# Feed-forward and output projections turned from features-on-partitions to tokens-on-partitions in a two-layer streaming trunk

## The chip, the cores and the metric

The kernel runs on one core of one Trainium2 chip. The metric is device microseconds for one execution, the median of three runs. The engines are named as in the profile: PE is TensorE's matmul, PEld its weight load, DVE VectorE, ACT ScalarE, POOL GpSimd, SP SyncE. SP and ACT also issue DMAs here.

## The reference

Two layers over 256 tokens of 2048 features, all in float32. Layer 0 is a gated and a pooled mixer, layer 1 a latent attention; each is followed by a gated feed-forward layer of 5632 hidden features. Everything but the matrix products that follow here is the same before and after.

```python
for layer in range(DEPTH):                     # 2
    h = rmsnorm(x, g_mix[layer])               # x: 256 x 2048
    if layer % 2 == 0:                         # mixers; w_out_ab is 2048 x 2048
        p = h @ w_in_ab[i]
        mix = concatenate([a, b]) @ w_out_ab[i]
    else:                                      # attention; w_out_c is 2048 x 2048
        mix = mla(h, w_in_c[i], ..., w_out_c[i], cos, sin)
    x = x + mix
    h = rmsnorm(x, g_ffn[layer])
    # w_gate, w_up: 2048 x 5632, w_down: 5632 x 2048
    x = x + (silu(h @ w_gate[layer]) * (h @ w_up[layer])) @ w_down[layer]
return rmsnorm(x, g_final)
```

## The kernel before

**Precision.** Every weight and every activation that meets it is held as two float32r parts whose sum is the float32 value. A weight is loaded as `raw` (1 MB a load), ACT copies it to `wh` (L90) and DVE subtracts to get `wl` (L91), 1024 columns at a time. `raw` has 3 buffers, `wh` and `wl` 4 each. Activations lie the same way, the high part in the first 256 columns of a tile, the low part in the next 256 (`split_into`, L145). A product is wh x hi + wh x lo + wl x hi.

**The form before (`column`, L95).** The trunk `x` and all activations have features on the 128 partitions and the 256 tokens along the columns. One 128 x 128 block of weights stands in the array, and the activations move through it: one matmul of 512 columns (wh against hi and lo side by side, L113) and one of 256 (wl against hi, L114). This pair is the unit of work; the last pair of a sum has the two the other way round (L110, L111). A column tile is 16 pairs (22 for half of a down projection) and gives 128 output features for all tokens. `gather_halves` (L137) adds the two halves that stand in PSUM.

**The other form (`token_major`, L205),** used before for the attention's values only (`w_v1`) and written out by hand for the gated mixer's v (L239 to L261): 128 tokens of an activation stand in the array and 512 weight columns move. For one 128-row slice of the weights and one half of the tokens it takes three matmuls of 512 columns: hi against wh, hi against wl, lo against wh (L217 to L219).

**Stages.** The mixer v (to 53 us), the other mixer inputs, the output projection `w_o0` (16 column tiles), the feed-forward of layer 0 (two halves of 22 hidden tiles, each gate and up column by column, then 16 column tiles of the down projection), the latent attention (its products of `w_ckv`, `w_kr` and `w_cq` by `column`), the output projection `w_o1`, the second feed-forward, the final norm. `residual` (L187) adds a column tile of PSUM to `x`, writes the split input `xs` of the next product and the squares for the norm. The norm's factor is applied to the result of the product: `rstd_of` sums squares over partitions by a matmul, `spread` lays the factor along the columns by another. The engines run their own rows in order; a scheduler lays down that order when the kernel is built, and semaphores connect the engines.

Of the kernel before, what the change touches and what calls it, by code (L numbers as in the profile page):

```python
# [11 lines left out]
ALU = mybir.AluOpType  # L12
# [5 lines left out]
KD = D // P            # 16 feature tiles of the trunk  # L18
DFF = 5632
NF = DFF // P          # 44 feature tiles of the feed-forward layer  # L20
HALF = NF // 2
# [4 lines left out]
SPLIT = 1024           # weights split at a time, per partition  # L26
# [3 lines left out]
def trunk(ctx: ExitStack, tc: tile.TileContext, a: dict, out: bass.AP):  # L30
# [14 lines left out]
    x = big.tile([P, KD, T], F32, name="x")  # L45
    xs = big.tile([P, KD, 2 * T], F32R, name="xs")

# [4 lines left out]
    cnt = const.tile([P, 16], F32, name="cnt")  # L52

# [15 lines left out]
    # the table of activation functions is fetched while the first loads are under way  # L69
    warm = const.tile([P, 1], F32, name="warm")  # L70
    nc.scalar.activation(out=warm, in_=ones[:, 0:1], func=AF.Gelu_apprx_tanh)
    # and the tensor engine's clock is brought up
# [5 lines left out]
    def split_weights(src, n):  # L78
        """[P, n] of DRAM as pairs of tiles whose sum is exactly the weights."""
        raw = raws.tile([P, 2 * SPLIT], F32, name="raw")  # L80
        nc.sync.dma_start(out=raw[:, :n], in_=src)
        return split_raw(raw, n)
# [12 lines left out]
    def column(w, nk, moving):  # L95
        """One 128-column tile of a product, transposed: [128, (hi + cross | lo)] in PSUM."""
        ps = ps_mm.tile([P, 2 * T], F32, name="mm")
        k = 0
        for o in range(0, nk * P, 2 * SPLIT):
            n = min(2 * SPLIT, nk * P - o)  # L100
            for wh, wl, m in split_weights(w[:, o:o + n], n):
                for j in range(m // P):
                    product(ps, wh[:, j * P:(j + 1) * P], wl[:, j * P:(j + 1) * P], moving[:, k, :], k == 0, k == nk - 1)
                    k += 1
        return ps

    def product(ps, wh, wl, mv, first, last):
        """wh x (hi | lo) into the two halves, wl x hi into the first; the matmul that ends the sum covers both."""
# [7 lines left out]
    def short_product(ps, wh, wl, mv, first, last):  # L116
        """As product(), all of it in ps[:, :T]: for sums of few terms, where adding halves would weigh."""
# [4 lines left out]
    def columns(w, nk, nm, moving):  # L122
        """Column tiles whose weights share a load: w is [P, nm * nk * 128]."""
# [13 lines left out]
    def gather_halves(ps, name):  # L137
        """ps[:, :T] + ps[:, T:] in SBUF."""
# [6 lines left out]
    def split_into(dst, src, scale=None):  # L145
        """dst[:, :T] + dst[:, T:] = src (times a gain per partition), both parts in float32r."""
# [8 lines left out]
    def add_square(acc, src, first):  # L155
        if first:
            nc.scalar.activation(out=acc, in_=src, func=AF.Square)
        else:
            sq = tmp.tile([P, T], F32, name="sq")
# [3 lines left out]
    def rstd_of(accs, n):  # L163
        """(mean + eps) ** -0.5 of sums of squares (over partitions and over accs), per token on the
        partitions. spread() lays it along the free axis, the same on every partition."""
# [21 lines left out]
    def residual(m, ps, g, acc):  # L187
        """x tile m += product; then what the next layer needs of it."""
        t = tmp.tile([P, T], F32, name="rs")
        nc.vector.tensor_tensor(out=t, in0=ps[:, :T], in1=x[:, m, :], op=ALU.add)  # L190
        nc.vector.tensor_tensor(out=x[:, m, :], in0=ps[:, T:], in1=t, op=ALU.add)  # L191
        if g is None:
            return
        if g == "final":
            if m == KD - 1:
                # the last squares go into the sum over partitions by themselves
                nc.scalar.activation(out=last_sq, in_=x[:, m, :], func=AF.Square)
            else:
                add_square(acc, x[:, m, :], m == 0)
            nc.scalar.activation(out=fin[:, m, :], in_=x[:, m, :], func=AF.Copy, scale=gain("final", m))  # L200
        else:
            split_into(xs[:, m, :], x[:, m, :], gain(g, m))
            add_square(acc, x[:, m, :], m == 0)

    def token_major(w, nk, ncols, moving, evict):  # L205
        """Products with tokens on the partitions: w is [ncols/512][P, nk, 512]."""
        for c in range(ncols // 512):
            pss = [ps_mm.tile([P, 512], F32, name="mm") for _ in range(2)]
            for k0 in range(0, nk, 4):
                parts = split_weights(w[c, :, k0 * 512:(k0 + 4) * 512], 2048)  # L210
                for k in range(k0, k0 + 4):
                    wh, wl, _ = parts[(k - k0) // 2]
                    s = slice((k - k0) % 2 * 512, (k - k0) % 2 * 512 + 512)
                    for t in range(2):
# [4 lines left out]
                        nc.tensor.matmul(pss[t], lhsT=lo, rhs=wh[:, s], start=False, stop=k == nk - 1)  # L219
            for t in range(2):  # L220
                evict(c, t, pss[t])
# [7 lines left out]
    # x times the final gain, and the squares of its last tile  # L229
    fin = last_sq = None  # L230

# [1 line left out]
    # the gated mixer's v, tokens on the partitions; its loads alternate with those of x  # L233
    vg = att.tile([P, 2, 1024], F32, name="ckv")
    vss = stat.tile([P, 2, 2], F32, name="vss")
    sums = big.tile([P, 8, T], F32, name="hid")
    acc, sq = sums[:, :4, :], sums[:, 4:, :]
    pss = [[ps_mm.tile([P, 512], F32, name="mm") for t in range(2)] for c in range(2)]
    for k0 in range(0, KD, 2):  # L239
        raw = raws.tile([P, 2 * SPLIT], F32, name="raw")  # L240
        if k0 == 0:
            for k in range(2):
                nc.sync.dma_start(out=x[:, k, :], in_=a["x"][:, k, :])
                for c in range(2 * k, 2 * k + 2):
                    nc.sync.dma_start(out=raw[:, c * 512:(c + 1) * 512], in_=a["w_v0"][0][:, c * 512:(c + 1) * 512])
        else:
            nc.sync.dma_start(out=x[:, k0:k0 + 2, :], in_=a["x"][:, k0:k0 + 2, :])
            nc.sync.dma_start(out=raw, in_=a["w_v0"][k0 // 2])
        step = SPLIT if k0 else 512
        for k in (k0, k0 + 1):  # L250
            split_into(xs[:, k, :], x[:, k, :], gain("mix0", k))
# [368 lines left out]
```

## Time and profile before

| | before |
|---|---|
| median of three runs | 2015.97 us (2014.3 to 2018.14) |
| span of the profiled execution | 2013.7 us |
| PE busy | 1998.8 us, 99% of the span |
| DVE / ACT busy | 64% / 49% |
| mean granted TensorE clock | 0.997 of full speed |
| HBM traffic | 364 MB read, 182 GB/s |

The span runs from the first to the last instruction. The time of the profiled execution beyond its span is not listed; the fastest of the three runs is 0.6 us above the span, the median 2.3 us. A matmul's listed duration overlaps its neighbours, so what it costs in a row of matmuls is the distance from one start to the next.

### The profile page before, as it was taken

What the parts mean: (1) busy time and instruction counts of PE and PEld (TensorE: products, weight loads), DVE (VectorE), ACT (ScalarE), POOL (GpSimd) and SP (SyncE); (2) the same over time, 40 slices, a digit from 0 to 9 for tenths busy, and PEclk for the clock granted to TensorE, in tenths of its full rate; (3) what the DMA queues carried; (4) which work ended last, traced back from release to release, by engine and by line L of the source; (5) the groups of instructions that cost most, each with busy time, mean ns of one, the idle gap of its engine ahead of it and who ended that gap; (6) DMA issues with size and microseconds to landing.
All of it is one profiled execution on the core that took longest, in us unless ns stands there. A gap on an engine that the chain in (4) does not pass through costs nothing.

```text
span 2013.7 us, 28325 instructions
## 1 busy us (share of the span) xinstructions
PE 1998.8 (99%) x11436; PEld 1740.6 (86%) x11436; DVE 1291.6 (64%) x1899; ACT 987.8 (49%) x1440; POOL 7.4 (0%) x22
## 2 busy tenths in 40 slices
PE   9999999999999999999999999999999999999997
PEld 7888888888888888888899988888888888888886
DVE  6787666666556666666676767666665566666654
ACT  6554454444334455444455655544543345554442
POOL 0000000000000000000000000000000000000000
PEclk9999999999999999999999999999999999999998
DMA  7565555555556555555555245555555565555553
GB/s 278 170 209 186 189 188 183 186 182 177 182 188 201 188 188 188 175 175 191 196 184 167 85 161 182 182 187 188 188 169 192 179 202 183 188 186 187 173 187 121
DMA packets 60179, 368.11 MB, mean 183 GB/s; under 512 B 6928, under 2 KB 8720, under 8 KB 19344
## 3 DMA queue, kind: packets, MB, share of 16 engines
q1 hardware_dynamic: 58320, 364.93, 55.0%
q8 instruction: 89, 1.46, 0.3%
q10 hardware_dynamic: 1728, 1.37, 0.2%
q14 instruction: 42, 0.34, 0.0%
HBM read 364.18 MB, written 2.10 MB: 182 GB/s over the span
## 4 chain that ended last, share of the span: by engine, by line
PE 97%; DVE 1%; DMA 1%; ACT 0%; issue 0%; SPq 0%; POOLq 0%; DVEq 0%; ACTq 0%
PE mm L113 56%; PE mm L114 28%; PE mm L111 3%; PE mm L110 2%; PE mm L119 1%; PE mm L120 1%; PE mm L118 1%; PE mm L260 1%; PE mm L261 1%; PE sm L466 1%; PE mm L259 1%; DMA raw<-in_w_v 1%; PE sm L465 0%; PE mm L218 0%; PE mm L219 0%; PE mm L217 0%
## 5 line engine op out<-in xcount | busy, mean ns | idle before, releaser
L91 DVE TENSOR_TENSOR wl<-raw,wh 128x1024 fp32r<-128x1024 f32 (+2 forms) x708 | 844.7, 1194 | 420.6 <-ACT wh L90 414.2
L113 PE MATMUL mm<-xs,wh 128*128 128x512 f32 x3015 | 1073.3, 399 | 0.0
L90 ACT ACTIVATE wh<-raw 128x1024 fp32r<-128x1024 f32 (+2 forms) x708 | 731.9, 1034 | 561.3 <-PE mm L113 322.1
L114 PE MATMUL mm<-xs,wl 128*128 128x256 f32 x3015 | 846.2, 281 | 0.0
L113 PEld LDWEIGHTS mm<-xs,wh 128*128 128x128 f32 x3015 | 566.5, 188 | 129.8
L113 PE MATMUL mm<-hid,wh 128*128 128x512 f32 x1824 | 648.8, 399 | 0.0
L114 PEld LDWEIGHTS mm<-xs,wl 128*128 128x128 f32 x3015 | 569.3, 189 | 8.8
L114 PE MATMUL mm<-hid,wl 128*128 128x256 f32 x1824 | 512.6, 281 | 0.0
L113 PEld LDWEIGHTS mm<-hid,wh 128*128 128x128 f32 x1824 | 342.7, 188 | 80.2 <-DVE hid L149 0.3
L114 PEld LDWEIGHTS mm<-hid,wl 128*128 128x128 f32 x1824 | 344.5, 189 | 4.6
L140 ACT ACTIVATE half<-mm 128x256 f32<-128x256 f32 x201 | 77.2, 384 | 373.3 <-PE mm L111 373.3
L142 DVE TENSOR_TENSOR su<-mm,half 128x256 f32<-128x256 f32 x88 | 37.4, 425 | 95.3 <-ACT half L140 95.3
L142 DVE TENSOR_TENSOR sg<-mm,half 128x256 f32<-128x256 f32 x88 | 37.4, 424 | 90.5 <-ACT half L140 90.5
L111 PE MATMUL mm<-xs,wh 128*128 128x512 f32 x201 | 80.3, 400 | 0.0
L190 DVE TENSOR_TENSOR rs<-mm,x 128x256 f32<-128x256 f32 x96 | 40.8, 424 | 46.9 <-PE mm L111 46.9
L110 PE MATMUL mm<-xs,wl 128*128 128x256 f32 x201 | 56.7, 282 | 0.0
L148 ACT ACTIVATE hid<-su 128x256 fp32r<-128x256 f32 x88 | 37.0, 420 | 39.4 <-DVE su L387 39.4
L110 PEld LDWEIGHTS mm<-xs,wl 128*128 128x128 f32 x201 | 37.8, 188 | 10.2
L191 DVE TENSOR_TENSOR x<-mm,rs 128x256 f32<-128x256 f32 x96 | 40.7, 424 | 3.3
L387 DVE TENSOR_TENSOR su<-su,sg 128x256 f32<-128x256 f32 x88 | 37.4, 425 | 3.3
L386 DVE TENSOR_TENSOR su<-su,rstd 128x256 f32<-128x256 f32 x88 | 37.4, 424 | 3.0
L383 DVE TENSOR_TENSOR sg<-sg,rstd 128x256 f32<-128x256 f32 x88 | 37.3, 424 | 2.9
(146 smaller groups left out, 1111.3 us busy)
## 6 DMA issues: line engine op xcount, KB each, us to landing
raw<-in_w_gu SPq DMA_DIRECT2D x176, 1024.0 KB, 5.1
raw<-in_w_d SPq DMA_DIRECT2D x64, 1024.0 KB, 4.9
raw<-in_w_o SPq DMA_DIRECT2D x32, 1024.0 KB, 4.9
raw<-in_w_d SPq DMA_DIRECT2D x64, 384.0 KB, 3.1
raw<-in_w_v SPq DMA_DIRECT2D x11, 1024.0 KB, 6.7
raw<-in_w_z SPq DMA_DIRECT2D x8, 1024.0 KB, 4.9
raw<-in_w_u SPq DMA_DIRECT2D x8, 1024.0 KB, 4.9
raw<-in_w_q SPq DMA_DIRECT2D x6, 1024.0 KB, 4.9
```

Source lines behind the costliest of these rows:

```text
L90: nc.scalar.activation(out=wh[:, :m], in_=raw[:, o:o + m], func=AF.Copy)
L91: nc.vector.tensor_tensor(out=wl[:, :m], in0=raw[:, o:o + m], in1=wh[:, :m].bitcast(F32), op=ALU.subtract)
L110: nc.tensor.matmul(ps[:, :T], lhsT=wl, rhs=mv[:, :T], start=False, stop=False)
L111: nc.tensor.matmul(ps, lhsT=wh, rhs=mv, start=False, stop=True)
L113: nc.tensor.matmul(ps, lhsT=wh, rhs=mv, start=first, stop=False)
L114: nc.tensor.matmul(ps[:, :T], lhsT=wl, rhs=mv[:, :T], start=False, stop=last)
L140: nc.scalar.activation(out=c, in_=ps[:, T:], func=AF.Copy)
L142: nc.vector.tensor_tensor(out=s, in0=ps[:, :T], in1=c, op=ALU.add)
L190: nc.vector.tensor_tensor(out=t, in0=ps[:, :T], in1=x[:, m, :], op=ALU.add)
L191: nc.vector.tensor_tensor(out=x[:, m, :], in0=ps[:, T:], in1=t, op=ALU.add)
L386: nc.vector.tensor_tensor(out=su, in0=su, in1=r, op=ALU.mult)
L387: nc.vector.tensor_tensor(out=su, in0=su, in1=sg, op=ALU.mult)
```

## The change

The gate, up, down and both output projections go over to the tokens-on-partitions form; the products of layer 1's inputs (`w_ckv`, `w_kr`, `w_cq`) and the mixer inputs keep the old one. The trunk `x` becomes [128 tokens, 2 halves, 2048]. What a product takes must still have features on the partitions, so the results are transposed on PE: `turned` makes four 128 x 128 float32 transposes into one PSUM tile, and ACT and DVE split them from there. These calls wait in a list, `pending`, and one is taken after each load of weights (four slices of 128 rows) in `token_major`, or after each fourth pair in `column`. The norm's sums now come from the squaring activation's accumulator, per token, so that `rstd_of` and `spread` leave the feed-forward layers and the end. The input comes a second time as `xt`, tokens on partitions (2 MB), and the final gain as a row broadcast to all partitions (1 MB), both issued by ACT. A feed-forward layer is cut into 6 and 5 blocks of 512 hidden features.

```diff
-    def token_major(w, nk, ncols, moving, evict):
-        for c in range(ncols // 512):
+    def token_major(w, k0, nk, blocks, moving, evict):
+        for c in blocks:
             pss = [ps_mm.tile([P, 512], F32, name="mm") for _ in range(2)]
...
                     for t in range(2):
                         hi = moving[:, k, t * P:(t + 1) * P]
                         lo = moving[:, k, T + t * P:T + (t + 1) * P]
                         nc.tensor.matmul(pss[t], lhsT=hi, rhs=wh[:, s], start=k == 0, stop=False)
                         nc.tensor.matmul(pss[t], lhsT=hi, rhs=wl[:, s], start=False, stop=False)
                         nc.tensor.matmul(pss[t], lhsT=lo, rhs=wh[:, s], start=False, stop=k == nk - 1)
+                next_pending()
+            evict(c, pss)
+
+    def turned(src, put):
+        pt = ps_sm.tile([P, 512], F32, name="sm")
+        for j in range(2):
+            for t in range(2):
+                o = j * T + t * P
+                nc.tensor.transpose(pt[:, o:o + P], src(t, j), ident)
+        put(pt)
+
+    def into_trunk(w, k0, nk, moving, g, sums):
+        def evict(c, pss):
+            s = slice(c * 512, (c + 1) * 512)
+            for t in range(2):
+                nc.vector.tensor_tensor(out=x[:, t, s], in0=pss[t], in1=x[:, t, s], op=ALU.add)
+            if g is None:
+                return
+            for t in range(2):
+                sq = qpool.tile([P, 512], F32, name="qr")
+                nc.scalar.activation(out=sq, in_=x[:, t, s], func=AF.Square, accum_out=sums[:, t, c:c + 1])
+            if g == "final":
+                for t in range(2):
+                    nc.vector.tensor_tensor(out=x[:, t, s], in0=x[:, t, s], in1=gfin[:, s], op=ALU.mult)
+                return
+            for m in (4 * c, 4 * c + 2):
+                def put(pt, m=m):
+                    for j in range(2):
+                        split_into(xs[:, m + j, :], pt[:, j * T:(j + 1) * T], gain(g, m + j))
+                pending.append(lambda m=m, put=put: turned(lambda t, j: x[:, t, (m + j) * P:(m + j + 1) * P], put))
+        token_major(w, k0, nk, range(4), moving, evict)
...
+    nc.scalar.dma_start(out=gfin, in_=a["g_final"].broadcast_to([P, D]))
+    nc.scalar.dma_start(out=x, in_=a["xt"])
...
-    for m in range(KD):
-        residual(m, column(a["w_o0"][m], KD, ab), "ffn0", acc)
+    into_trunk(a["w_o0"], 0, KD, ab, "ffn0", sums)
...
-                pg = column(wgu[f, :, 0:D], KD, xs)
-                pu = column(wgu[f, :, D:2 * D], KD, xs)
...
+                def evict_gate(c, pss):
+                    for t in range(2):
+                        sg = qpool.tile([P, 512], F32, name="qn")
+                        nc.scalar.activation(out=sg, in_=pss[t], func=AF.Silu, scale=r[:, t:t + 1])
+                        gate.append(sg)
+                def evict_up(c, pss, hid=hid, at=at):
+                    hd = att.tile([P, 2, 512], F32, name="ckv")
+                    for t in range(2):
+                        nc.vector.scalar_tensor_tensor(out=hd[:, t, :], in0=pss[t], scalar=r[:, t:t + 1], in1=gate[t],
+                                                       op0=ALU.mult, op1=ALU.mult)
+                    for m in (0, 2):
...
+                        pending.append(lambda m=m, put=put: turned(lambda t, j: hd[:, t, (m + j) * P:(m + j + 1) * P], put))
+                token_major(wg, 0, KD, [c], xs, evict_gate)
+                token_major(wu, 0, KD, [c], xs, evict_up)
+            into_trunk(wd, 4 * at, 4 * n, hid, g_next if part else None, after)
...
-    rps = spread(rstd_of([acc, last_sq], D))
+    r = trunk_rstd(feed_forward(1, sums, "final"))
+    for t in range(2):
+        for o, n in ((0, 512), (512, 512), (1024, 1024)):
+            y = x[:, t, o:o + n]
+            if o < 1024:
+                nc.vector.tensor_scalar(out=y, in0=y, scalar1=r[:, t:t + 1], scalar2=None, op0=ALU.mult)
+            else:
+                nc.scalar.activation(out=y, in_=y, func=AF.Copy, scale=r[:, t:t + 1])
+            nc.sync.dma_start(out=out[:, t, o:o + n], in_=y)
```

Three places in the order of the instructions follow; an x and a number behind a row count equal rows that follow each other.

On PE, in the first feed-forward layer before, the join of two column tiles of a down projection:

```order
L114 MATMUL mm<-hid,wl 128x256
L110 MATMUL mm<-hid,wl 128x256
L111 MATMUL mm<-hid,wh 128x512
L113 MATMUL mm<-hid,wh 128x512
L114 MATMUL mm<-hid,wl 128x256
```

On PE in the changed kernel, the first load of a down projection's first block (24 matmuls) ends, and the four transposes of the last hidden block (`ckv` is the buffer that holds it) stand ahead of the second load:

```order
L211 MATMUL mm<-wl,hid 128x512
L212 MATMUL mm<-wh,hid 128x512
L222 MATMUL sm<-ident,ckv 128x128 x4
L210 MATMUL mm<-wh,hid 128x512
L211 MATMUL mm<-wl,hid 128x512
```

The 512 and 256 column pairs with weights in the array gave way to threes of 512 columns, and 68 such groups of four transposes have come in.

On ACT before, two hidden tiles of a feed-forward layer (`wh` the split of weights, `half` the gathering of gate and up, `sg` the gate's activation, `hid` the split of the result):

```order
L90 ACTIVATE wh<-raw 128x1024
L384 ACTIVATE sg<-sg 128x256
L90 ACTIVATE wh<-raw 128x1024
L140 ACTIVATE half<-mm 128x256
L90 ACTIVATE wh<-raw 128x1024
L148 ACTIVATE hid<-su 128x256
```

On ACT now, a gate and an up block of 512 hidden features (`qn` the gate's activation, read from the gate's PSUM; `hid` the split of two transposed tiles, read from the transposes' PSUM):

```order
L94 ACTIVATE wh<-raw 128x1024 x3
L417 ACTIVATE qn<-mm,rtok 128x512 x2
L94 ACTIVATE wh<-raw 128x1024 x11
L429 ACTIVATE hid<-sm 128x2x256
L94 ACTIVATE wh<-raw 128x1024 x2
L429 ACTIVATE hid<-sm 128x2x256
```

Of the 8 splits of the up block three now stand ahead of the gate's activation, which waits for the end of the gate block; before, such a wait came with every column tile, about every second split.

On ACT before, the first rows of the kernel that touch loads:

```order
L271 DMA rope_c<-in_rope_c 128x256
L90 ACTIVATE wh<-raw 128x512 x2
L151 ACTIVATE xs<-x,gains 128x256
L272 DMA rope_s<-in_rope_s 128x256
L90 ACTIVATE wh<-raw 128x512 x2
```

And now (`gfin` the broadcast final gain; the 2 MB of `x<-in_xt` follow eleven rows further on, after eight of the sixteen slices' `xs`):

```order
L304 DMA rope_c<-in_rope_c 128x256
L94 ACTIVATE wh<-raw 128x512 x2
L162 ACTIVATE xs<-hid,gains 128x256
L305 DMA rope_s<-in_rope_s 128x256
L94 ACTIVATE wh<-raw 128x512
L306 DMA gfin<-in_g_final 128x2048
L94 ACTIVATE wh<-raw 128x512
```

The broadcast of 1 MB has moved in among the first splits of weights, while the first loads of weights are under way.

## Rows read from the trace of the kernel before

**Rows 1.** The page's first part: busy time, share of the span, instructions.
```profile
PE 1998.8 (99%) x11436; PEld 1740.6 (86%) x11436; DVE 1291.6 (64%) x1899; ACT 987.8 (49%) x1440; POOL 7.4 (0%) x22
```

**Rows 2.** The chain that ended last, shares by engine; then PE's longest wait after 1172 us.
```profile
PE 97%; DVE 1%; DMA 1%; ACT 0%; issue 0%; SPq 0%; POOLq 0%; DVEq 0%; ACTq 0%
...
PE sm L169 <- ACT ssq_q L197: 1.3, 1, 1.3
```

**Rows 3.** Windows 500 to 800 us, L113's, then L111's matmuls: length, PE, PEld, clock, DMA.
```profile
500.00:800.00 300.00, 284.94 (x802) 150.62 (x802) 1.00 0.58 190
500.00:800.00 300.00, 19.20 (x48) 9.12 (x48) 1.00 0.58 190
```

**Rows 4.** Timeline of PE, tokens-on-partitions products: mixer v, then attention's values (start, duration).
```profile
15.87 0.40 PE L261 MATMUL mm<-wh,xs 128*128 128x512 f32 x1
...
52.61 0.39 PE L261 MATMUL mm<-wh,xs 128*128 128x512 f32 x1
...
1066.57 0.40 PE L217 MATMUL mm<-wh,ckv 128*128 128x512 f32 x1
...
1088.35 0.28 PE L118 MATMUL mm<-hid,wh 128*128 128x256 f32 x1
```

**Rows 5.** The attention's transposes (L486): their durations, and PE's timeline around two of them.
```profile
L486 PE MATMUL sm<-ident,pr x48: 270/272/315, 1102.2 to 1166.0; 128*128 128x128 f32 x48
...
1163.40 0.40 PE L113 MATMUL mm<-hid,wh 128*128 128x512 f32 x1
1163.64 0.27 PE L486 MATMUL sm<-ident,pr 128*128 128x128 f32 x1
1163.66 0.37 PE L114 MATMUL mm<-hid,wl 128*128 128x256 f32 x1
1163.87 0.38 PE L486 MATMUL sm<-ident,pr 128*128 128x128 f32 x2
1164.01 0.47 PE L113 MATMUL mm<-hid,wh 128*128 128x512 f32 x1
1164.32 0.28 PE L114 MATMUL mm<-hid,wl 128*128 128x256 f32 x1
```

**Rows 6.** Timeline of ACT at a block's end in the attention's values: start, duration, idle before.
```profile
1076.99 1.37 ACT L456 ACTIVATE xs<-mm,rtok 128x512 f32<-128x512 f32 x2 [0.98 <-PE mm L219]
1078.26 1.05 ACT L90 ACTIVATE wh<-raw 128x1024 fp32r<-128x1024 f32 x1
```

**Rows 7.** Groups of DVE and ACT, shapes apart: busy, mean ns of one, idle before.
```profile
L91 DVE TENSOR_TENSOR wl<-raw,wh 128x1024 fp32r<-128x1024 f32 x636 | 777.8, 1224 | 331.3 <-ACT wh L90 325.0
L304 DVE TENSOR_TENSOR pa<-qn 128x512 f32<-128x512 f32 x4 | 2.8, 694 | 0.1
L283 ACT ACTIVATE qr<-ckv 128x512 f32<-128x512 f32 x4 | 2.5, 634 | 0.0
```

**Rows 8.** The chain that ended last, 53 to 60 us: a sum of squares, a spread factor.
```profile
53.00 0.34 PE sm L169 x4
59.10 0.44 PE sm L179 x4
```

**Rows 9.** A window (length, PE, PEld, DVE, ACT, POOL, clock, DMA, GB/s), then the chain there.
```profile
10.00:15.00 5.00, 4.62 (x20) 3.52 (x19) 1.35 (x3) 2.87 (x4) 0.00 (x0) 1.00 1.01 379
...
6.54 6.52 DMA raw<-in_w_v
13.16 1.07 ACT wh L90
```

**Rows 10.** Timeline of the end: last add, POOL's power, store issues; then stores' KB and landing.
```profile
2000.40 0.42 DVE L190 TENSOR_TENSOR rs<-mm,x 128x256 f32<-128x256 f32 x1 [5.98 <-PE mm L111]
2003.03 0.69 POOL L173 TENSOR_TENSOR rtok<-rstd_v,mhalf 128x2 f32<-128x2 f32 x1 [742.50 <-DVE rstd_v L171]
2005.48 4.65 SPq L536 DMA_DIRECT2D out<-xs  x6
...
out<-xs SPq DMA_DIRECT2D x3, 512.0 KB, 2.9
```

## What I predicted, before the changed kernel ran

> **What bounds the kernel now.** I read the page's busy times first: PE is busy 99% of the span, DVE 64%, ACT 49% [rows 1]. Then the chain of waits that ended last: 97% of it is PE, and from 1172 us on PE waits longest for the last squares, 1.3 us at the very end [rows 2]. So a stage costs what its matmuls cost on PE, and whatever ACT, DVE or a load needs is hidden as long as it stays ahead. DMA is at 0.58 in the feed-forward, with the granted clock at 1.00, full speed [rows 3]. The edit must therefore be judged by PE's time per unit of product, then by what is new on PE, then by places where a cover could go.
>
> **The products.** The listed duration of a matmul (about 0.4 us for 512 columns) overlaps the next one, so the price is the distance between starts. Before, windows 500 to 800 us hold 802 pairs by L113 and 48 by L111, 850 pairs in 300 us: 0.353 us a pair [rows 3]. This includes every join of two column tiles. The changed form is in the trace twice. The mixer v has 163 matmuls from 15.87 to 52.61 us, 162 distances, 0.2268 us each; the attention's values have 96 from 1066.57 to 1088.35 us, 0.2269 each [rows 4]. The first has the same xs in the array as the gate and up products will have, the second has four block ends in it, so a join makes it no longer.
> Pairs that change: two output projections of 16 x 16 blocks (512) and six feed-forward products of 16 x 44 (4224), 4736 in all. They took 4736 x 0.353 = 1671.8 us. Four pairs (128 rows by 512 outputs, 256 tokens) become six matmuls of 512 columns: 4736 / 4 x 6 = 7104, x 0.2268 = 1611.2 us. **Saved: 60.6 us.** The number of columns that move is equal (4 x 768 = 6 x 512 = 3072); what goes is one instruction in four, 9472 to 7104.
>
> **The transposes.** There are 68 groups of four: 44 for 22 hidden blocks, 24 for three passages of the trunk into a next product. That is 272. Row L486 lists 0.272 us for the same instruction, but again the start distances count: from L113 at 1163.40 to L114 at 1164.32 are 0.92 us, in which stand two L113, one L114 and three transposes; a pair is 0.353, an L113 alone some 0.235, so three transposes took 0.92 - 0.353 - 0.235 = 0.33 us, 0.11 each, in the middle of float32r matmuls of both sizes [rows 5]. 272 x 0.11 = **29.9 us added**. Bounds: 0.10 to 0.16 each (the upper one a little over half of the listed duration, if a group cost something at its two ends), 27 to 44 us.
>
> **What leaves PE besides.** Two feed-forward layers lose a sum (0.34) and a spread (0.44), the entry of layer 1 a sum [rows 8]: **1.9 us saved**.
>
> **Joins and waits.** The new waits are ACT's gate activation and DVE's up product, which wait for a block's end with later splits queued behind them in order, and PE's transposes, which wait for DVE's result. At a block's end three splits of the next block stand ahead of the gate's activation, so PE has 1.5 loads, 36 matmuls or 8.2 us, in hand. In the attention's values the same happens: ACT waits 0.98 us for the end of a block, evicts in 1.37 us and then splits [rows 6], and the distance there stayed 0.2269. Per 24 matmuls (5.44 us) DVE has two splits of 1.224 us and ACT two of 1.05, plus four operations of 512 columns at some 0.69 in eight such stretches [rows 6, 7], about half of the time. The transposes come 5.4 us after a block's end; two DVE operations of 0.69 are done after 1.5. So nothing is late and I put these at nothing; if the cover were gone, each of 68 blocks would pay up to a split by ACT and DVE, 2.3 us. The load rate rises from 1 MB in 16 pairs (5.65 us) to 1 MB in 5.44, DMA from 0.58 to 0.60: no bound.
> One place is tighter: layer 1's entry, where `column` takes its first transposes 1.4 us after the down projection ends and needs the split tiles at its 13th pair, 4.2 us plus 0.9 of transposes later. DVE's two adds (1.4), ACT's two squares (0.64 each) and four splits of 0.4 to 0.5 with a weight split between come to about 5. I take **0.5 us**, between 0 and 2.
>
> **The start.** PE waits there for a load: the chain goes through 6.52 us of one `w_v` load, with DMA at 1.01 and 379 GB/s [rows 9]. The broadcast of 1 MB is now issued by ACT during that load. At 379 GB/s it takes 2.8 us; if the queues share evenly the load is late by up to that. The 2 MB of `xt` come later, when PE already runs without a gap (from 15.87 us on, [rows 4]). Bounds 0 (all hidden) and 8.3 (all 3 MB in front of PE); a gain is excluded, since nothing is taken from the queues. I take **2 us added**, near the first load's share.
>
> **The end.** Before, from the last add's start at 2000.40 to 2013.7 are 13.3 us: two adds, squares, a matmul over partitions, POOL's power (0.69), a spread, scaling and stores [rows 10]. Now: two adds of 512 (0.69 each, the nearest DVE row), the second square (0.64), the second gain product (0.69), two small DVE operations (about 0.3), POOL 0.7 with 0.3 to reach it, two ACT scalings of 1.05: the last store is issued some 6.6 us after the start, and 512 KB land 2.9 us later [rows 6, 7, 10]; 2 MB at 400 GB/s from the first store at 4.9 end about as late. With the 0.8 us that before lies between the last landing and the end, 10.5 to 12 us. I take **2 us saved** (0 to 3.5).
>
> **The sum** against the profiled execution: 2013.7 - 60.6 + 29.9 - 1.9 + 0.5 + 2 - 2 = 1981.6 us of span. The median of the runs lies 2.3 us above the span before; with the same distance 1983.9, and since more of my unknowns add than save I round to **1985**.
>
> **Rivals.** (1) *The 512-column form costs what an L113 costs.* In a pair the 512 columns take some 0.235 us. If the changed stages showed that and not 0.2268, 7104 x 0.235 = 1669.4, nothing would be saved and the transposes would be paid: 2013.7 - 2.4 + 29.9 - 1.9 + 0.5 = 2039.8, with 2.3 about **2042**, slower. It decides from 0.231 us on, where the saving equals 30 us. Against it: two stages and 259 matmuls at 0.2268 [rows 4].
> The Trainium skill ("TensorE: Matmul & The Clock Gate", section "Back-to-back issue gap") gives columns / 2.4 GHz plus some 2.5 ns for matmuls back to back. By it the change would only save 2368 fixed parts of 2.5 ns, an estimate of 6 us, less than the transposes cost, about 2036 us of span. The trace differs: 0.353 a pair and 0.2268 a matmul are 28 and 11 ns above what the page gives, so more goes with each instruction than the page allows.
> (2) *A transpose holds PE for its listed duration.* 272 x 0.272 = 74.0 us in place of 29.9 gives 1981.6 + 44.1 + 2.3 = **2028**, slower. It decides from 0.22 us each on. Against it: three of them in 0.33 us [rows 5].
> The same page, section "Part 4: PE-mode transpose", tells of about 275 ns for a transpose in a kernel. The listed 272 agrees; the start distances of 0.11 say that most of it overlaps.
> (3) *The joins.* If in-order ACT or DVE made PE wait at each of 68 block ends, 1 us each would give **2053**, and 0.46 us each (31 us) is where the gain is gone. Against it: PE has no wait at the four block ends of [rows 4], and three splits stand ahead. For it: ACT and DVE still run in order, and an eviction is now two operations of 512 columns.
> (4) *The start costs all 3 MB*, 8.3 us: **1991**, still faster.
>
> **How the numbers follow.** Forecast 84%, its own range 1978 to 1994; rival 1 3%, rival 2 4%, rival 3 4% (a third of it below 2012), rival 4 5%. The range 1977 to 2000 takes in the bounds: transposes at 0.10 to 0.16 (-3 to +14), the end (-1.5 to +2), the start (-2 to +6), the entry (to +1.5); it leaves out rivals 1, 2 and most of 3 and some of the tails. A measurement of this kernel can tell about 0.2%, 4 us. Faster by more: the forecast, rival 4 and a part of 3, 0.90; within 0.2%: 0.02; slower: 0.08.
>
> **What would show it.** Right: 7200 matmuls of 512 columns in `token_major` (96 of them the attention's values) with starts 0.227 us apart in the feed-forward; L222's 272 transposes some 0.11 apart, and the matmul after a group not late; no PE wait for ACT or DVE between 60 us and the end beyond a microsecond; a start later by about 2 us, seen as the first unbroken stretch of PE; some 11 us from the last product to the end. Wrong: distances of 0.235, transposes of 0.2 or more, or a PE wait that returns with every block. If the span falls by less than 25 us, one of these must show; if by more than 40, the transposes hide or a pair's successor is cheaper than in the rows.

## The result and the profile after

| | before | after |
|---|---|---|
| median | 2016.57 us (2014.3 to 2018.14) | **1985.07 us** (1984.43 to 1986.36) |
| ratio of after to before | | **0.9845**, 95% interval 0.9832 to 0.9859 |
| span of the profiled execution | 2013.7 us | 1983.8 us |
| PE busy | 1998.8 us, x11436 | 1966.6 us, x9308 |
| DVE / ACT busy | 64% / 49% | 54% / 46% |

The same kernel, run again beside the last experiment below, gave 1984.26 us (1983.09 to 1986.05) against 2015.4, again 0.9845 (0.9832 to 0.9859), and a profiled span of 1981.3. The forecast was 1985, between 1977 and 2000.

**What bounds it now** is still PE. From the page after, the busy times (answer to [rows 1]) and the chain that ended last, by engine and by line (to [rows 2]):

```profile
PE 1966.6 (99%) x9308; PEld 1646.5 (83%) x9308; DVE 1069.0 (54%) x1250; ACT 907.2 (46%) x1144; POOL 7.4 (0%) x22
PE 97%; DVE 1%; DMA 1%; ACT 0%; issue 0%; ACTq 0%; SPq 0%; POOLq 0%; POOL 0%
PE mm L212 27%; PE mm L210 27%; PE mm L211 27%; PE mm L124 4%; PE mm L125 2%; PE sm L222 1%; PE mm L131 1%; PE mm L130 1%; PE mm L129 1%; PE mm L293 1%; PE mm L294 1%; DMA raw<-in_w_v 1%; PE sm L510 1%; PE mm L292 1%; PE sm L509 0%; DVE wl L95 0%
```

L210 to L212 are the three matmuls of `token_major`, L222 is the new transpose, L124 and L125 are the pair of `column`, which had been L113 and L114.

**The products.** PE's groups between 500 and 800 us of after (line, tiles, shapes, count, busy us and mean ns of one, idle time before them), and that window's row (busy time and count of each engine, granted clock, DMA share, GB/s), which answer [rows 3]:

```profile
L210 PE MATMUL mm<-wh,xs 128*128 128x512 f32 x244 | 95.5, 391 | 0.0
L212 PE MATMUL mm<-wh,xs 128*128 128x512 f32 x245 | 95.4, 389 | 0.0
L211 PE MATMUL mm<-wl,xs 128*128 128x512 f32 x244 | 94.9, 389 | 0.0
L210 PE MATMUL mm<-wh,hid 128*128 128x512 f32 x192 | 74.9, 390 | 0.0
L212 PE MATMUL mm<-wh,hid 128*128 128x512 f32 x192 | 74.7, 389 | 0.0
L211 PE MATMUL mm<-wl,hid 128*128 128x512 f32 x192 | 74.7, 389 | 0.0
L222 PE MATMUL sm<-ident,ckv 128*128 128x128 f32 x32 | 4.8, 272 | 0.0
500.00:800.00 300.00, 300.00 (x1341) 248.46 (x1340) 148.52 (x133) 123.83 (x125) 0.00 (x0) 1.00 0.56 192
```

The first six groups are 1309 matmuls. A window counts every matmul that touches it, also the two that had begun before 500 us, so 1307 begin in it; with some 3.6 us taken off for 32 transposes, 296.4 / 1307 = 0.2268 us each, as forecast (between two neighbours of 512 columns the starts are 0.2267 apart on average). No group has idle time before it.

**The transposes.** PE after, start and duration in us, a group of four in the first feed-forward layer (answer to [rows 5]):

```profile
183.16 0.40 PE L212 MATMUL mm<-wh,hid 128*128 128x512 f32 x1
183.39 0.60 PE L222 MATMUL sm<-ident,x 128*128 128x128 f32 x4
183.75 0.48 PE L210 MATMUL mm<-wh,hid 128*128 128x512 f32 x1
184.07 0.39 PE L211 MATMUL mm<-wl,hid 128*128 128x512 f32 x1
```

Such a matmul is listed with 0.48 and not 0.39, so the group is measured to the start of the one behind it: 183.39 to 184.07 are 0.68 us, of which one matmul of 512 columns is 0.227; the other 0.453 are four transposes, 0.113 each. The 66 such groups that stand among threes of 512 columns gave 0.110 to 0.112. The page lists 0.272 for each, as before.

**The waits.** All that PE waited for an engine in after, first from 60 us to the end, then before 60 us (who waited for whom: us in total, times, longest):

```profile
PE sm L510 <- DVE qr L560: 0.7, 3, 0.3
PE mm L292 <- ACT wh L94: 2.7, 3, 1.9
PE sm L79 <- DVE ones L68: 1.0, 1, 1.0
```

The first is inside the attention. None belongs to a block's end, none to a transpose. At layer 1's entry only a weight load waits, 0.3 us for DVE's split.

**The stages.** PE's first matmul of the output projections and of layer 1's inputs, and the last product, in after:

```profile
156.07 0.47 PE L210 MATMUL mm<-wh,hid 128*128 128x512 f32 x1
978.11 0.39 PE L124 MATMUL mm<-xs,wh 128*128 128x512 f32 x1
1145.58 0.47 PE L210 MATMUL mm<-wh,hid 128*128 128x512 f32 x1
1971.23 0.39 PE L212 MATMUL mm<-wh,hid 128*128 128x512 f32 x1
```

The same four in before:

```profile
152.59 0.47 PE L113 MATMUL mm<-hid,wh 128*128 128x512 f32 x1
990.12 0.40 PE L113 MATMUL mm<-xs,wh 128*128 128x512 f32 x1
1156.35 0.47 PE L113 MATMUL mm<-hid,wh 128*128 128x512 f32 x1
1999.96 0.40 PE L111 MATMUL mm<-hid,wh 128*128 128x512 f32 x1
```

| stretch | before, us | after, us | difference |
|---|---|---|---|
| to `w_o0` | 152.6 | 156.1 | +3.5 |
| `w_o0` and first feed-forward | 837.5 | 822.0 | -15.5 |
| layer 1's inputs and attention | 166.2 | 167.5 | +1.2 |
| `w_o1` and second feed-forward | 843.6 | 825.7 | -18.0 |
| from the last product to the end | 13.7 | 12.6 | -1.2 |

All of the gain is in the two stretches that changed form; the other three together cost 3.5 us. Layer 1's stretch holds two of the groups of transposes, 0.9 of its 1.2.

**The start.** PE after at the first wait for a load, and at the end of the mixer v (L180):

```profile
13.42 0.39 PE L294 MATMUL mm<-wh,xs 128*128 128x512 f32 x1
15.67 1.20 PE L292 MATMUL mm<-wh,xs 128*128 128x512 f32 x4 [1.86 <-ACT wh L94]
17.29 0.63 PE L294 MATMUL mm<-wh,xs 128*128 128x512 f32 x1
17.72 0.63 PE L293 MATMUL mm<-wl,xs 128*128 128x512 f32 x1
20.68 0.40 PE L293 MATMUL mm<-wl,xs 128*128 128x512 f32 x1
55.86 0.50 PE L180 MATMUL sm<-ones,hid 128*128 128x1 f32 x4
```

The mixer v ended at 52.84 us before, so this profile is 3.0 us later. The chain of waits goes through the same load as in [rows 9], which took longer (start, duration):

```profile
6.21 8.24 DMA raw<-in_w_v
```

PE waits 1.86 us for the copy of that load, and behind that the matmuls start 0.43 us apart until 20.7 us. The windows 15 to 20 and 20 to 25 us (columns as in the window row above):

```profile
15.00:20.00 5.00, 4.27 (x12) 3.10 (x13) 3.58 (x5) 3.71 (x6) 0.00 (x0) 0.72 1.02 424
20.00:25.00 5.00, 5.00 (x22) 4.08 (x21) 3.69 (x5) 4.78 (x7) 0.00 (x0) 0.94 1.02 417
```

They show why: the granted clock was 0.72 and 0.94 there, and 0.50 from 18 to 20 us, so for a few microseconds it stood at its lower level, 1.2 GHz, after PE's gap. In before the gap is 0.38 us at that place and both windows have 1.00. So the 3.0 us have two parts: the load landed 1.4 us later (at 14.45 and not at 13.06), and the eight matmuls at the lower clock took 1.6 us more.

**The end**, DVE, ACT and SP from the last product on (answer to [rows 10]):

```profile
1970.98 1.37 DVE L230 TENSOR_TENSOR x<-mm,x 128x512 f32<-128x512 f32 x2 [7.88 <-PE mm L212]
1972.46 1.37 DVE L238 TENSOR_TENSOR x<-x,gfin 128x512 f32<-128x512 f32 x2
1974.25 0.69 POOL L253 TENSOR_TENSOR rtok<-rstd_s,mhalf 128x2 f32<-128x2 f32 x1 [728.25 <-DVE rstd_s L251]
1974.97 2.19 ACT L580 ACTIVATE x<-x,rtok 128x1024 f32<-128x1024 f32 x2 [1.87 <-POOL rtok L253]
1975.49 3.71 SPq L581 DMA_DIRECT2D out<-x  x6
```

### The profile page after: what moved, and what is told of

The parts are those of the page before. It is cut to its first block, busy times and chain, and to the rows that moved or that the text cites. A ratio compares the mean times of both kernels' runs of the same rounds, so it can differ in the third digit from the quotient of the medians.

```text
span 1983.8 us, 22969 instructions
## 1 busy us (share of the span) xinstructions
PE 1966.6 (99%) x9308; PEld 1646.5 (83%) x9308; DVE 1069.0 (54%) x1250; ACT 907.2 (46%) x1144; POOL 7.4 (0%) x22
## 4 chain that ended last, share of the span: by engine, by line
PE 97%; DVE 1%; DMA 1%; ACT 0%; issue 0%; ACTq 0%; SPq 0%; POOLq 0%; POOL 0%
PE mm L212 27%; PE mm L210 27%; PE mm L211 27%; PE mm L124 4%; PE mm L125 2%; PE sm L222 1%; PE mm L131 1%; PE mm L130 1%; PE mm L129 1%; PE mm L293 1%; PE mm L294 1%; DMA raw<-in_w_v 1%; PE sm L510 1%; PE mm L292 1%; PE sm L509 0%; DVE wl L95 0%
## 5 line engine op out<-in xcount | busy, mean ns | idle before, releaser
L95 DVE TENSOR_TENSOR wl<-raw,wh 128x1024 fp32r<-128x1024 f32 (+1 forms) x692 | 843.1, 1219 | 839.7 <-ACT wh L94 839.1
L94 ACT ACTIVATE wh<-raw 128x1024 fp32r<-128x1024 f32 (+1 forms) x692 | 729.6, 1055 | 937.7 <-PE mm L212 864.6
L210 PE MATMUL mm<-wh,xs 128*128 128x512 f32 x1408 | 551.6, 392 | 0.0
L212 PE MATMUL mm<-wh,xs 128*128 128x512 f32 x1408 | 548.1, 389 | 0.0
L211 PE MATMUL mm<-wl,xs 128*128 128x512 f32 x1408 | 547.7, 389 | 0.0
L210 PE MATMUL mm<-wh,hid 128*128 128x512 f32 x960 | 376.7, 392 | 0.0
L212 PE MATMUL mm<-wh,hid 128*128 128x512 f32 x960 | 374.0, 390 | 0.0
L212 PEld LDWEIGHTS mm<-wh,xs 128*128 128x128 f32 x1408 | 264.2, 188 | 55.3
L210 PEld LDWEIGHTS mm<-wh,xs 128*128 128x128 f32 x1408 | 264.4, 188 | 53.4
L212 PEld LDWEIGHTS mm<-wh,hid 128*128 128x128 f32 x960 | 180.2, 188 | 38.0
L210 PEld LDWEIGHTS mm<-wh,hid 128*128 128x128 f32 x960 | 180.2, 188 | 36.2
L124 PE MATMUL mm<-xs,wh 128*128 128x512 f32 x375 | 134.4, 400 | 0.0
L125 PE MATMUL mm<-xs,wl 128*128 128x256 f32 x375 | 105.0, 280 | 0.0
L124 PEld LDWEIGHTS mm<-xs,wh 128*128 128x128 f32 x375 | 70.5, 188 | 16.0 <-DVE xs L163 0.3
L125 PEld LDWEIGHTS mm<-xs,wl 128*128 128x128 f32 x375 | 70.9, 189 | 0.5
L417 ACT ACTIVATE qn<-mm,rtok 128x512 f32<-128x512 f32 x44 | 29.9, 689 | 19.6 <-PE mm L212 19.6
L162 ACT ACTIVATE xs<-sm,gains 128x256 fp32r<-128x256 f32 x48 | 22.3, 466 | 30.5 <-DVE xs L163 30.5
```

The lines of the kernel that those rows point to most:

```text
L94: nc.scalar.activation(out=wh[:, :m], in_=raw[:, o:o + m], func=AF.Copy)
L95: nc.vector.tensor_tensor(out=wl[:, :m], in0=raw[:, o:o + m], in1=wh[:, :m].bitcast(F32), op=ALU.subtract)
L124: nc.tensor.matmul(ps, lhsT=wh, rhs=mv, start=first, stop=False)
L125: nc.tensor.matmul(ps[:, :T], lhsT=wl, rhs=mv[:, :T], start=False, stop=last)
L162: nc.scalar.activation(out=dst[:, :T], in_=src, func=AF.Copy, scale=scale)
L210: nc.tensor.matmul(pss[t], lhsT=hi, rhs=wh[:, s], start=k == 0, stop=False)
```

## The experiments

Ratios are to the kernel before, run on the same chip beside the experiment.

**The transposes left out** (of after).

```diff
 def turned(src, put):
-    pt = ps_sm.tile([P, 512], F32, name="sm")
-    for j in range(2):
-        for t in range(2):
-            o = j * T + t * P
-            nc.tensor.transpose(pt[:, o:o + P], src(t, j), ident)
-    put(pt)
+    put(src(0, 0))
...
```

> The changed kernel without the 272 transposes on PE: ACT and DVE split the untransposed results straight from SBUF, with as many operations of the same size, so the output is another one. Theory (a transpose costs the distance between starts, 0.11 us, and its neighbours nothing): 272 x 0.112 = 30 us less than the changed kernel, about 1955 us. Rival (each holds PE for its listed 0.272 us): 74 us less, about 1911. Rival (they hide beside the products): about 1985, as it is.

1952.65 us (1951.61 to 1953.89), ratio 0.9688 (0.9675 to 0.9701), span 1951.6, which is 32.2 us below that of after. In the window 500 to 800 us 1323 matmuls of 512 columns begin, 0.2268 each; in after 16 fewer begin there for its 32 transposes, 3.6 us, 0.113 each. The theory of 0.11 holds; the listed duration (74 us) and free transposes (0) both fall.

**The new loads issued late** (of after): the gain row and `xt` by SP behind the first loads of the mixer inputs.

```diff
-    nc.scalar.dma_start(out=gfin, in_=a["g_final"].broadcast_to([P, D]))
-    nc.scalar.dma_start(out=x, in_=a["xt"])
...
+    nc.sync.dma_start(out=gfin, in_=a["g_final"].broadcast_to([P, D]))
+    nc.sync.dma_start(out=x, in_=a["xt"])
     for m in range(8):
```

> The broadcast final gain and the token-major input are issued by SP after the first loads of the mixer inputs, and no longer by ACT during the mixer v. Theory (the mixer v ends 3.0 us later than before because the 3 MB share the DMA with its loads): the stage ends at 52.8 us again, the whole is 3 us shorter, about 1982 us. Rival (the start is late for another reason, such as the other order on ACT): stage end near 55.9, about 1985.

1984.21 us (1983.19 to 1984.59), ratio 0.9844 (0.983 to 0.9857). The mixer v ended at 54.70 us, not at 52.8; PE's gap there was 2.67 us and the granted clock 0.66 from 15 to 20 us. Nothing that can be told from after.

**Only the gain row late** (of after), `xt` left among ACT's issues.

```diff
-    nc.scalar.dma_start(out=gfin, in_=a["g_final"].broadcast_to([P, D]))
...
+    nc.sync.dma_start(out=gfin, in_=a["g_final"].broadcast_to([P, D]))
     for m in range(8):
```

> The final gain alone is issued late, the token-major input stays on ACT during the mixer v. Theory (the 1 MB of the gain makes one load late and PE's gap then costs clock): the mixer v ends at about 52.8 us, span about 1981. Rival (the 2 MB count too): between 53.5 and 55.9 us.

1987.11 us in one execution; the mixer v ended at 57.66, later than in after. But `xt` didn't stay where it was in time: with the gain row gone from ACT's issues it moved up. Its issue in after, then here:

```profile
20.83 0.34 ACTq L307 DMA_DIRECT2D x<-in_xt  x1
7.61 0.35 ACTq L306 DMA_DIRECT2D x<-in_xt  x1
```

So this kernel put 2 MB where after has 1 MB, beside the first loads of weights, and is no test of the gain row alone. That its mixer v ended later than in any other run of the changed kernel with four buffers would fit a delay by the loads beside it, but it is one execution.

What the two together can say is limited by what came later. The second profile of the unchanged after ended its mixer v at 53.58 us, and the last kernel below, which again has both loads late, at 56.19. The load that PE waits for and the row of the mixer v's end, in the profile of each:

```profile
5.81 6.72 DMA raw<-in_w_v
53.58 0.50 PE L180 MATMUL sm<-ones,hid 128*128 128x1 f32 x4
```

```profile
6.35 8.55 DMA raw<-in_w_v
56.19 0.50 PE L180 MATMUL sm<-ones,hid 128*128 128x1 f32 x4
```

So with the loads early it was 53.58 and 55.86, with both late 54.70 and 56.19. In the profiles that have the loads of before it was 51.65 to 54.13 (before and four experiments made from it). The start of after is later by some 2 us on average, but moving the two loads away doesn't bring it back. What the traces do show is where the time lies. From the landing of that load to the end of the mixer v are 39.8 us in all five profiles with the start of before, and 41.0, 41.4, 41.1 and 41.3 in these four (after twice, both loads late twice). Some 1.2 to 1.6 us thus go behind the landing, where the granted clock was down in these four. The rest is the landing itself: 11.8 to 14.3 us in the five with the start of before, 12.5 and 14.5 in after, 13.6 and 14.9 with both loads late. Why the clock fell there, and why that load lands when it does, stays open.

**Every second pair with its 256 columns first** (of before).

```diff
...
-        if last and not first:
+        if odd:
             nc.tensor.matmul(ps[:, :T], lhsT=wl, rhs=mv[:, :T], start=False, stop=False)
-            nc.tensor.matmul(ps, lhsT=wh, rhs=mv, start=False, stop=True)
+            nc.tensor.matmul(ps, lhsT=wh, rhs=mv, start=False, stop=last)
```

`odd` is `k % 2`, k the number of the pair in its sum.

> The kernel before, with every second pair turned round, so that the sizes come as 512, 256, 256, 512. Theory (each matmul costs its columns plus some 13 ns, and a further 3 ns goes at each change between the two sizes, since 0.2268 + 0.120 is 6 ns less than the 0.353 of a pair): half of the changes go, 5136 x 3.2 ns = 16 us less than before, about 2000 us. Rival (the 6 ns belong to the form of the 512-column matmul over activations): no change, about 2016.

1992.4 us (1990.55 to 1993.67), ratio 0.9884 (0.9871 to 0.9898), span 1990.0: 23.7 us gained with not one instruction less, three quarters of what the whole change brings. PE's groups with `xs` from 500 to 800 us:

```profile
L113 PE MATMUL mm<-xs,wh 128*128 128x512 f32 x273 | 107.9, 395 | 0.0
L111 PE MATMUL mm<-xs,wh 128*128 128x512 f32 x272 | 107.6, 396 | 0.0
```

With those on `hid` they are 862 pairs in 300 us, 0.348 each in place of 0.353. The size of the effect was underestimated, and it turned the question round: how much of what the change saves comes from its fewer instructions?

**Groups of four** (of before): four matmuls of 512, eight of 256, eight of 512, and so on.

```diff
+                for j0 in range(0, m // P, 4):
+                    group = range(j0, min(j0 + 4, m // P))
+                    for part in ("h", "l") if (k + j0) // 4 % 2 == 0 else ("l", "h"):
+                        for j in group:
...
```

`"h"` is the matmul of 512 columns with wh, `"l"` the one of 256 with wl.

> The kernel before, with the matmuls of a column tile in groups of four: four of 512 columns, four of 256, then four of 256, four of 512, and so on, the same matmuls in another order. Before, sizes change twice a pair (0.353 us), with every second pair turned once a pair (0.348 us); here they change once in four pairs. Theory A (each change costs some 4.7 ns): 0.3445 us a pair, 5136 x 8.2 ns = 42 us less than before, about 1974 us, below the changed kernel. Theory B (the sum of columns plus 13 ns each, 0.3467, is the floor): 31 us less, about 1984. Rival (the turned order helped for another reason than the changes): as with every second pair turned, about 1992.

1996.61 us (1995.73 to 1998.53), ratio 0.9908 (0.9891 to 0.9924), span 1994.3. About as good as the order above, a little worse, where a price for each change of size would have made it clearly better. In its runs of eight a matmul of 512 columns took 0.230 us on average and one of 256 took 0.119.

**All 512** (of before): wl meets both halves of the activations, so every matmul has 512 columns.

```diff
...
-            nc.tensor.matmul(ps[:, :T], lhsT=wl, rhs=mv[:, :T], start=False, stop=last)
+        nc.tensor.matmul(ps, lhsT=wh, rhs=mv, start=first, stop=False)
+        nc.tensor.matmul(ps, lhsT=wl, rhs=mv, start=False, stop=last)
```

> The kernel before with one more term: the low part of the weights meets high and low parts of the activations in one matmul of 512 columns, in place of 256. So each pair is two matmuls of 512 columns, activations moving, each with its own weights, and no size changes. Theory A (a matmul of 512 columns costs what it costs in the changed kernel, and the mix of sizes is what a pair pays for): 2 x 0.2266 = 0.453 us a pair, 662 pairs in the window 500 to 800. Theory B (it is the form: with activations moving 512 columns cost more whatever stands beside them): 2 x 0.235 = 0.470 us, 638 pairs. Between, 2 x 0.230 = 0.460, 652 pairs, as in the runs of eight of the grouped order.

Its span is 2529.7 us, which doesn't matter here; the window does. PE's groups from 500 to 800 us:

```profile
L109 PE MATMUL mm<-hid,wh 128*128 128x512 f32 x352 | 136.9, 389 | 0.0
L110 PE MATMUL mm<-hid,wl 128*128 128x512 f32 x352 | 136.9, 389 | 0.0
L109 PE MATMUL mm<-xs,wh 128*128 128x512 f32 x311 | 121.0, 389 | 0.0
L110 PE MATMUL mm<-xs,wl 128*128 128x512 f32 x311 | 121.0, 389 | 0.0
```

They are 1326, of which 1324 begin in the 300 us, **0.2267 apart**: the price of the changed kernel, with activations moving. Theory A holds. The form has no price of its own.

**All 256** (of before): the matmul of 512 columns cut in two, except in the first and last pair of a sum.

```diff
...
-            nc.tensor.matmul(ps, lhsT=wh, rhs=mv, start=first, stop=False)
-            nc.tensor.matmul(ps[:, :T], lhsT=wl, rhs=mv[:, :T], start=False, stop=last)
+            nc.tensor.matmul(ps[:, :T], lhsT=wh, rhs=mv[:, :T], start=False, stop=False)
+            nc.tensor.matmul(ps[:, T:], lhsT=wh, rhs=mv[:, T:], start=False, stop=False)
+            nc.tensor.matmul(ps[:, :T], lhsT=wl, rhs=mv[:, :T], start=False, stop=False)
```

> The kernel before with the matmul of 512 columns cut in two of 256, except in the first and last pair of a sum: 14 of 16 pairs (20 of 22) are three matmuls of 256 columns, again with no change of size within them, and one instruction more in each. Theory A (each instruction costs its columns at 2.4 GHz and a fixed part, which is 0.2266 - 0.2133 = 0.013 us in the changed kernel): 3 x 0.120 = 0.360 us, 2 per cent above the pair of before. Theory B (a matmul of 256 columns costs the 0.116 us it shows beside one of 512, and the change of size is what costs): 0.348 us, below the pair of before although it has an instruction more.

2043.09 us in one execution. PE, two rows that stand 21 distances apart:

```profile
604.20 0.28 PE L116 MATMUL mm<-hid,wh 128*128 128x256 f32 x1
...
606.71 0.28 PE L116 MATMUL mm<-hid,wh 128*128 128x256 f32 x1
```

2.51 / 21 = 0.120 us each, 0.359 for three: theory A's 0.360, and not theory B's 0.348.

**Two buffers for wh and wl** (of after) in place of four, to take the cover from the joins.

```diff
-    whs = pool("whs", 4)
-    wls = pool("wls", 4)
+    whs = pool("whs", 2)
+    wls = pool("wls", 2)
```

> The changed kernel with 2 buffers each for the split weights in place of 4, so that at a block's end PE holds half a load of split weights where it had one and a half. Theory (the joins cost nothing because splits stand ahead): PE now waits at the joins, some 0.5 to 2 us at each of 68, 10 to 60 us more, 1995 to 2045. Rival (the joins would cost nothing in any case): about 1985.

2021.56 us in one execution, span 36 us above after. But PE's waits between 270 and 1010 us, which holds the first feed-forward, are only these:

```profile
PE mm L211 <- DVE wl L95: 0.5, 1, 0.5
PE mm L210 <- ACT wh L94: 0.2, 1, 0.2
```

They stand one load behind a single join, of 30 there, and make 0.7 us; the second feed-forward has the same two. Most of the loss is ahead of it, in the mixer, which still runs in `column`: `w_o0` starts at 186.29 us and not at 156.07. Its window from 60 to 160 us (columns as before):

```profile
60.00:160.00 100.00, 83.24 (x447) 71.81 (x446) 61.30 (x117) 42.07 (x72) 2.28 (x8) 0.91 0.40 141
```

After has 100.00 and x594 there. So for the feed-forward the theory of a price at each join falls even with half the buffers; it is the mixer that can't do with two.

**Matmuls to fill the gap at the start** (of after): ten small ones in the mixer v.

```diff
+        if k0 == 0:
+            fill = ps_sm.tile([P, 512], F32, name="sm")
+            for _ in range(10):
+                nc.tensor.matmul(fill[:, :P], lhsT=ones, rhs=ones, start=True, stop=True)
```

> The changed kernel with ten 128-column float32 matmuls on a spare PSUM tile among the first slices of the mixer v, so that PE has work while it waits for the second load. Theory (half of the later start comes from the granted clock, which fell to half for 3.4 us behind PE's gap of 1.9 us): the clock stays at full there, the mixer v ends about 1.6 us sooner, near 54.3 us. Rival (the fall of the clock has nothing to do with the gap): the stage ends at 55.9 or later.

1984.72 us in one execution. They were laid ahead of the gap, from 9.96 us on; the gap of 2.51 us stayed and so did the lower clock (0.66 from 15 to 20 us). Inconclusive.

**Late loads and the better order of pairs together** (of after, for the 400 pairs that still run in `column`), beside after itself:

> The changed kernel as it is, to stand on the same chip beside the next one. Expected 1985 us, ratio 0.984 to the kernel before.

> The changed kernel with the two edits that were worth something alone: gfin and xt issued by SP behind the first mixer-input loads, and, in what is left of `column` (400 pairs of the mixer inputs and layer 1's inputs), every second pair with its 256 columns first. Theory A (the gains are per pair and per load, so they add up): 400 pairs x (0.353 - 0.348) = 2 us, and 1.2 us of the start, about 1982, 3 us below the changed kernel. Theory B (what the order of pairs was worth belonged to the feed-forward's long rows of pairs, or the gain of the start is absorbed): 1984 to 1985, nothing that can be told from the changed kernel.

1982.59 us (1981.29 to 1984.4), ratio 0.9835 (0.9822 to 0.9849), against 1984.26 and 0.9845 (0.9832 to 0.9859) for after on the same chip. The median is 1.7 us lower, near theory A, but the intervals overlap for most of their length: not shown to be faster than after.

## Why the prediction was right, point by point

**Products: right in size, with a cause that the prediction only half named.** Forecast 7104 matmuls at 0.2268, saving 60.6. By their starts they were 0.2267, 1610.5 us; and of the 850 pairs that the prediction counts in the window of [rows 3] 849 begin in it, 0.3533 each, so the pairs had cost 1673.2 and not 1671.8. Saved: 62.7. The prediction put this down to one instruction in four that goes, and in rival 1 it took 0.235 as the price that the other form might have. The two uniform kernels separate the parts. In long rows of one size 512 columns cost 0.2267, whichever operand moves, and 256 columns 0.120 (seen with activations moving only). A pair at these prices would be 0.3467; before it was 0.3533. So of the 62.7 us about 4736 x 0.0066 = 31 us were the mix of two sizes, and only the other 31 (4736 x 0.3467 - 1610.5) the fewer instructions. The transposes cost about as much as the fewer instructions saved, so what the change gains in all, 30 us, is about what the mix had cost. The 0.235 of rival 1 was the price of 512 columns beside 256, not of a form; it would not have come with it.

Why an alternating pair costs more is not settled. In before the matmul of 512 columns is the dear one (its next starts some 0.236 later), the one of 256 is even cheap (0.117). With half the changes of size 0.005 of the 0.007 us came back, but with an eighth of them, in the groups of four, no more than that.

0.2267 and 0.120 are 13 ns above 512 and 256 columns at 2.4 GHz (0.2133 and 0.1067), the same for both. The Trainium skill ("TensorE: Matmul & The Clock Gate", section "Back-to-back issue gap") has this form, columns over the clock and a fixed part of some 2.5 ns, for an isolated matmul. The form agrees here and the figure doesn't. For a stream in which each matmul has its weight load, as here, the section gives about 131 ns at 512 columns; the windows from 500 to 800 us of seven kernels here have no two starts of 512 columns less than 225 ns apart.

**Transposes: right.** Forecast 0.11 each, 29.9 us; measured 0.110 to 0.113 by the distances, 272 x 0.112 = 30.5 us, and 32.2 us by leaving them out. Rival 2 would have made 74. The 272 ns of the listing mislead.

**Joins: right.** Nothing was forecast, and PE has no wait at any of them. Rival 3 fell twice, in after and with half the buffers.

**Layer 1's entry:** forecast 0.5, measured 0.3.

**Start: right within its bounds, with a cause that isn't shown.** Forecast +2 for a share of the broadcast; measured +3.0 in the first profile and +0.7 in the second. That the broadcast delays the load was the argument; with it and `xt` moved away the start stayed late, so this isn't borne out. The lower clock behind PE's gap was not in the sum at all: eight matmuls at 0.43 in place of 0.23 us make 1.6 of the 3.0, and the other 1.4 are the later landing. That +2 lies between the two profiles is luck. Rival 4 (8.3 us) fell.

**End:** forecast -2, with some 11 us from the last product on; measured -1.2 and 12.6. Two adds (1.37), two gain products (1.37), 0.5 us of small DVE operations, POOL, then the scaling: the first store is issued 4.3 us after the last product's start (1975.49 - 1971.23), and the other 8.3 us are scaling and stores.

**The sum.** With measured terms: -62.7 + 30.5 - 1.9 + 0.3 + 3.0 - 1.2 = -32.0 us; the span fell by 29.9. (The 1.9 of the norm's sums were not measured apart.) Some 2 us are in no term. The stretch to `w_o0` has 0.5 of them beyond the start; and without the transposes the span fell by 1.7 us more than their 30.5, which may be most of the rest, but nothing here shows at which place. That the median meets the forecast to 0.1 us is luck: the span came out 2.2 us above the forecast 1981.6, and the median stood only 1.3 us above that span, where the prediction had allowed 2.3 and rounded up by another 1.1.

## What to carry to other kernels

When PE is full, count what its instructions cost by the distance of their starts, in rows of the same neighbours: 512 columns were 0.227 us in a row of their own kind and 0.236 beside 256. Before a trunk is turned round, try the order of what is there: reversing every second pair gave 24 us here with an edit of four lines, where turning the trunk round gave 30. Transposes on PE in a stream of matmuls cost 0.11 us each and not the 0.27 they are listed with, so 272 of them took half of what the new form saved.

## What the runs showed that was not expected

- The order of matmuls of two sizes alone moves this kernel by 1.2% (0.9884), with the same instructions, columns and sums.
- In every profile with the start of after, PE waits 1.9 to 3.7 us for the copy of one load, and behind that the granted clock is down (0.66 to 0.73 in the window 15 to 20 us), with matmuls of 512 columns 0.43 us apart. With the start of before that window has 1.00 in five of five, also in the all-256 kernel, where PE had waited 1.77 us; the groups of four had such a fall earlier (0.80 from 5 to 10 us, behind a wait of 1.20 us). So the lower clock followed a wait each time, but not each wait brought it.
- The start differs from one execution to the next by more than moving both loads changed it: 53.58 and 55.86 us for the same kernel, 54.70 and 56.19 with the loads late.
